# A second buffer for raw weight rows, and a residual requested later, in a two-layer MLP

## The chip, the cores and the metric

The kernel runs on 1 core of one Trainium2 chip. The metric is the device time of one execution in microseconds; the median of several runs is compared.

## The reference

The program is one post-norm layer of an encoder on x (1024 tokens x 1024, float32): layer norm, an input projection, two groups of heads (a gated DeltaNet in both directions, and 2-D neighbourhood attention), an output projection, a residual with layer norm, and a squared-ReLU MLP with the same kind of residual. The change lies in the MLP, where D_FF = 4096 and alpha = 2^(1/4):

```python
mix = jnp.einsum('bte,ed->btd', jnp.concatenate([o_gdn, o_na], axis=-1), w_out[l])
x = layer_norm(DEEPNORM_ALPHA * x + mix, ln1_g[l], ln1_b[l])
ff = jnp.square(jax.nn.relu(jnp.einsum('btd,df->btf', x, w1[l]) + b1[l]))
ff = jnp.einsum('btf,fd->btd', ff, w2[l]) + b2[l]
x = layer_norm(DEEPNORM_ALPHA * x + ff, ln2_g[l], ln2_b[l])
```

## The kernel before, in words

Every product is made of three matmuls on float32r operands, each value split into a high part (an ACT copy) and the remainder (a VectorE subtraction, `sub_split`, line 71). Both layers of the MLP are written as seven products of half-size blocks in place of eight (a Strassen scheme), so sums and differences of blocks of the weights and of the activations are operands too.

First layer, `up_pair(g)` for g = 0 to 15 (line 1044): each g takes 256 columns of w1. `w1_raw` (line 887) requests 1 MB of raw w1 rows into a `q8` buffer (two of them), two groups ahead in the program. `w_steps` (line 895) makes four sums s1 to s4 in tiles of the tag `tt` (line 870) and seven split operands in tiles of the tag `y` (line 882, eight of them). The products are p6, p7, p5, p2, p4, p3; the one in `p3` (`psF`) reuses a PSUM bank which line 1101 (`join7`, tile `u`) has to read first. The activated blocks and their four sums are written to DRAM (`h_d`, lines 1042 and 1142). Ahead of the loop, six early pieces of w1 (`w1q`, lines 958 to 961) are loaded into `tt` tiles as well.

Within the same loop the sums of w2 that the second layer needs are made, half a group at a time: `w2_load` (line 1023) requests two pieces of 256 KB into the tile `r` (named w2r), of which there is one; `w2_sums` (line 1030) makes four sums on VectorE in the tile `t` (w2s), of which there is one too, and writes them to DRAM (`t_d`, line 1036, requested by ACT).

Second layer: seven products i, each in four groups, n = 4i + gr. `down_ops(n)` (line 1153) requests 1 MB of activations and 1 MB of weights (line 1163) into a `q8` pair where n is a multiple of 3, else into one of two `big` buffers, and splits them on ACT (line 1166) and VectorE into `x` tiles (five). The `big` buffers hold operands of the first layer until its last group's p4 and p3. `down_mm` (line 1262) makes 12 matmuls of 128 x 512 for each of four row blocks, 48 in a group. `take` (line 1238) adds the results of a product into the tiles `yr`. `down_ops` stands two groups ahead of its matmuls in the loop; groups 0 and 1 are requested within the last `up_pair` (`first_ops`).

The residual: after the first layer norm x goes to DRAM (`y_d`, line 941). Lines 1183 to 1194, which stand in the program between the two layers, request five vectors broadcast to all partitions (ln1's g and b, b2, ln2's g and b) in a pool that takes the place of the first layer's work tiles, and the eight tiles of `y_d` into `yr` (tag `y`, the buffers of the first layer's split weights); VectorE then makes alpha * (g y + b) + b2 of them.

What sets the order: all these loads are issued by SP, in order, on one queue; stores of h_d and t_d by ACT on its own. The order of each engine's instructions is not that of the program text. The kernel is built with `tile.TileContext(nc, schedule_with_timeline_sim=True)` (line 1378): a planner takes, for each engine, whichever instruction its own timing says is ready (operands there, a buffer free), earlier program lines first. On the chip the order is then fixed, and each engine waits at whatever is not ready. Paced matmuls and a few `issue_after` blocks add edges by hand, none of them at the lines of this change.

Of the kernel before, what the change touches and what calls it, by code (L numbers as in the profile page):

```python
# [7 lines left out]
F32 = mybir.dt.float32  # L8
F32R = mybir.dt.float32r
AF = mybir.ActivationFunctionType  # L10
ALU = mybir.AluOpType
# [4 lines left out]
P = 128  # L16
T = 1024
DM = 1024
NK = DM // P
NT = T // P  # L20
DFF = 4096
NF = DFF // P
ALPHA = 2.0 ** 0.25
# [13 lines left out]
def tile_trunk(ctx: ExitStack, tc: tile.TileContext, A: dict, out: bass.AP):  # L37
    nc = tc.nc
    V, S, G, TE, D = nc.vector, nc.scalar, nc.gpsimd, nc.tensor, nc.sync
# [3 lines left out]
    def open_pool(name, **kw):  # L43
        opened.append(tc.alloc_tile_pool(name=name, bufs=1, **({} if kw.get("space") == DRAM else {"reuse_waits": "tile"}), **kw))
        return opened[-1]
# [24 lines left out]
    def sub_split(eng, lo, full, hi):  # L70
        return eng.tensor_tensor(lo, full, f32(hi), ALU.subtract)  # L71
# [473 lines left out]
    for i in range(8):  # L545
        for d in range(2):
            n = i if d == 0 else 7 - i
            on = oaccs[n // 4][:, n % 4]
            ld = []
            for nm, src in (("vt", vt_d), ("kT", kT_d), ("qk", qk_d[d]), ("qT", qT_d), ("kt", kt_d)):  # L550
                t = p2.tile([P, 4, P], F32, tag="l" + nm, name="l" + nm, bufs=2)
# [129 lines left out]
    yp = open_pool("yacc")  # L681
# [107 lines left out]
    def raw8():  # L789
        return op.tile([P, 2, DM], F32, tag="q8", name="wraw", bufs=2)  # L790
# [32 lines left out]
    for p in range(4):  # L823
# [11 lines left out]
        for u in units[p]:  # L835
            if u == 8:
                r = [raw8() for i in range(2)]
                wo1 = load_wo(1, [r[k // 2][:, k % 2] for k in range(4)])
            t = u % 8
# [16 lines left out]
    y_d = dr.tile([NT, P, DM], F32, name="y_d")  # L856

    xp = open_pool("xops")
    wk = open_pool("work")
# [7 lines left out]
        X[nm] = bigp.tile([P, 2, 4, 512], F32R, tag="big", name="x" + nm, bufs=2)  # L867

    def tmp(name):
        return wk.tile([P, 512], F32, tag="tt", name=name, bufs=6)  # L870

    def hold8(name):
        return wk.tile([P, 512], F32, tag="f0", name=name, bufs=8)
# [21 lines left out]
    def w_steps(raw, w):  # L895

        q11, q12, q21, q22 = (w_quad(raw, a, k) for a in range(2) for k in range(2))
        s1, s2, s3, s4 = (tmp(f"ws{i}").rearrange("p (k c) -> p k c", k=4) for i in range(4))

        def put(nm, src):  # L900
            if nm not in w:
                w[nm] = w_split(src)

        V.tensor_tensor(s1, q21, q22, ALU.add)
        put("11", q11)
        yield
        V.tensor_tensor(s2, s1, q11, ALU.subtract)
        put("S2", s2)
        yield
        V.tensor_tensor(s3, q11, q21, ALU.subtract)  # L910
        put("S3", s3)
        yield
        put("S1", s1)
        yield
        put("12", q12)
        yield
        put("22", q22)
        yield
        V.tensor_tensor(s4, q12, s2, ALU.subtract)
        put("S4", s4)  # L920
        yield
# [36 lines left out]
    for g in range(1, NE):  # L958
        for k in range(2):
            rawq[g, k] = tmp("w1q").rearrange("p (k c) -> p k c", k=4)  # L960
            D.dma_start(rawq[g, k], A["w1"][k * 512:k * 512 + 512, 2 * g * P:(2 * g + 1) * P].rearrange("(kt p) c -> p kt c", p=P))
    for hf in range(2):
        for q in range(4):
            t = hf * 4 + q
# [52 lines left out]
    w2p = open_pool("w2p")  # L1017
# [3 lines left out]
    raws1[1] = w1_raw(1)  # L1021

    def w2_load(g, hc):
        r = w2p.tile([P, 2, 2, 256], F32, tag="r", name="w2r", bufs=1)
        for k in range(2):
            D.dma_start(r[:, k], A["w2"][(2 * g + k) * P:(2 * g + k + 1) * P, :]
                        .rearrange("p (j c) -> p j c", j=2)[:, :, hc * 256:hc * 256 + 256])
        return r
# [15 lines left out]
    def up_pair(g, mid=None):  # L1044
# [11 lines left out]
        else:  # L1056
# [3 lines left out]
            S.activation(u2, pa, AF.Copy)  # L1060
        step()
        r = w2_load(g - 1, 0) if g else None
        u3 = utile("u3")
        h11, h21, h22, h12 = (hold8(x) for x in ("h11", "h21", "h22", "h12"))
# [50 lines left out]
        if g == 0:  # L1115
            pe, pf = p5(), p3()
            pc = p7()
            p6()
            join7(pc)
            join5(pe)  # L1120
            p4()
            p2()
            join3(pf)
        else:
            p6()
            join7(p7())
            join5(p5())
            w2_sums(g - 1, 0, r)
            r = w2_load(g - 1, 1)
            if mid is not None:  # L1130
                mid()
            p2()
            p4()
            w2_sums(g - 1, 1, r)
            join3(p3())
# [17 lines left out]
    def down_ops(n):  # L1153
        i, gr = divmod(n, NQ)
        sl = slice(gr * 4, gr * 4 + 4)
        if n % 3 == 0:
            raws = [raw8().rearrange("p a (k c) -> p (a k) c", c=512) for j in range(2)]
        else:
            r = bigp.tile([P, 2, 4, 512], F32, tag="big", name="d2r", bufs=2)
            raws = [r[:, j] for j in range(2)]  # L1160
        res = []
        for src, raw in zip(order[i], raws):
            D.dma_start(raw, src[:, sl])
            t = xp.tile([P, 2, 4, 512], F32R, tag="x", name="d2", bufs=5)
            for k in (slice(0, 2), slice(2, 4)):
                S.activation(t[:, 0, k], raw[:, k], AF.Copy)  # L1166
                sub_split(V, t[:, 1, k], raw[:, k], t[:, 0, k])
            res.append(t)
        ops2[n] = res
# [7 lines left out]
    for hc in range(2):  # L1177
        w2_sums(NG - 1, hc, w2_load(NG - 1, hc))
# [2 lines left out]

    fp = open_pool("fin")
    gB, bB, g2B, b2L, b2B = (fp.tile([P, DM], F32, name=x) for x in ("gB", "bB", "g2B", "b2L", "b2B"))
    for t_, nm in ((gB, "ln1_g"), (bB, "ln1_b"), (b2B, "b2"), (g2B, "ln2_g"), (b2L, "ln2_b")):
        D.dma_start(t_, A[nm].to_broadcast([P, DM]))
    V.tensor_scalar(gB, gB, ALPHA, None, ALU.mult)
    V.scalar_tensor_tensor(bB, bB, ALPHA, b2B, ALU.mult, ALU.add)
    yr = []
    for t in range(NT):
        y = yp.tile([P, DM], F32, tag="y", name="yr", bufs=8)  # L1190
        D.dma_start(y, y_d[t])
        V.tensor_tensor(y, y, gB, ALU.mult)
        V.tensor_tensor(y, y, bB, ALU.add)
        yr.append(y)
    us = [fp.tile([P, 512], F32, name=f"us{q}") for q in range(4)]
    sts = {}

# [40 lines left out]
    def take(i, q, ps):  # L1238
        y0, y1, u = yr[q], yr[4 + q], us[q]
        if i == 0:  # L1240
            S.activation(u, ps, AF.Copy)
            add(y0[:, lo_], y0[:, lo_], ps)
        elif i == 1:
            add(u, u, ps)
            add(y0[:, hi_], y0[:, hi_], u)
        elif i == 2:
            add(u, u, ps)
            add(y1[:, lo_], y1[:, lo_], u)
        elif i == 3:
            add(y0[:, hi_], y0[:, hi_], ps)  # L1250
            add(u, u, ps)
            add(y1[:, hi_], y1[:, hi_], u)
            stats(4 + q, 512, 512)
        elif i == 4:
            add(y1[:, lo_], y1[:, lo_], ps)
            stats(4 + q, 0, 512)
            finish(4 + q, 0)
        elif i == 5:
            add(y0[:, lo_], y0[:, lo_], ps)
            stats(q, 0, 512)  # L1260

    def down_mm(ps, n, q, c, start, stop):
        h, w = ops2[n]
        qs_ = slice(q * P, (q + 1) * P)
        for k in range(4):
            TE.matmul(ps, h[:, 0, k, qs_], w[:, 0, k, c], start=(start and k == 0), stop=False)  # L1266
            TE.matmul(ps, h[:, 0, k, qs_], w[:, 1, k, c], start=False, stop=False)  # L1267
            TE.matmul(ps, h[:, 1, k, qs_], w[:, 0, k, c], start=False, stop=(stop and k == 3))  # L1268

    cuts = {q: ((0, 512),) for q in range(4)}  # L1270
    for i in range(7):
        if i == 6:
            cuts[3] = ((0, 256), (256, 256))
        tags = "st" if i % 2 == 0 else "op"
        ps = {}
        for q in range(4):
            for k, (c0, cn) in enumerate(cuts[q]):
                ps[q, c0] = psC.tile([P, cn], F32, tag="o" if k else tags[q // 2], name="psdn", bufs=2)
        for gr in range(NQ):
            n = i * NQ + gr  # L1280
            if n + 2 < 7 * NQ:
                down_ops(n + 2)
            if i == 6 and gr >= NQ - 2:
                continue
            for q in range(4):
                for c0, cn in cuts[q]:
                    down_mm(ps[q, c0], n, q, slice(c0, c0 + cn), gr == 0, gr == NQ - 1)
            if gr == NQ - 1:
                for q in range(4):
                    take(i, q, ps[q, 0])  # L1290
# [91 lines left out]
```

## Time and profile before

| what | us |
|---|---|
| median of 3 runs | 1384.3 |
| the three runs | 1372.8, 1384.89, 1384.3 |
| the profiled execution, its own time | 1387.8 |
| its span, first to last instruction | 1385.8 |
| PE (matmuls) busy | 1293.7 (93%) |
| DVE (VectorE) busy | 947.9 (68%) |
| ACT (ScalarE) busy | 634.3 (46%) |
| mean DMA rate over the span | 194 GB/s |

PE busy means that matmuls are in flight, and their ends are modelled. Times in the rows are microseconds from the start of the span unless they say ns. In a timeline the columns are start, duration, engine, line, operation, tile written <- tiles read, count (xN: N merged instructions), and in brackets the idle time ahead of it and what ended it. PEclk is TensorE's granted clock as a share of full speed. Arrows in tables of waits read "who <- whom it waited for: total us, times, longest". SP's and ACT's queue entries (SPq, ACTq) are the issuing of DMAs, not the transfers.

### The profile page before, as it was taken

How to read it: one execution, taken by the hardware profiler on the slowest of the kernel's cores; microseconds unless marked ns; L12 is line 12 of the kernel's file. 1: busy time of each engine (PE TensorE's matmuls, PEld its weight loads, DVE VectorE, ACT ScalarE, POOL GpSimd, SP SyncE). 2: the span in 40 equal slices, each digit the busy share in tenths (PEclk: the TensorE clock that was granted, in tenths of full speed). 3: DMA queues.
4: the chain of work that ended last, by engine and by line, in shares of the span. 5: the costliest groups of instructions: out<-in, count | busy, mean ns of one | idle time of the engine just before them, and what ended most of it. 6: DMA issues, size and time to landing. Idle time of an engine off the chain costs nothing. (4 is left out here: it accounts for less than half of the span.)

```text
span 1385.8 us, 20027 instructions
## 1 busy us (share of the span) xinstructions
PE 1293.7 (93%) x7318; PEld 1072.5 (77%) x7318; DVE 947.9 (68%) x1707; ACT 634.3 (46%) x1224; POOL 187.8 (14%) x208
## 2 busy tenths in 40 slices
PE   5999999999999977699998899999998999999996
PEld 4688888888888866688875687777786788888885
DVE  6755797942348645757699886777875686565855
ACT  5457666434333145346366454444444433333531
POOL 3000001011113237513130000000000000000403
PEclk9999999999999999899999899999999899999998
DMA  6134548466877599565154677677779957555721
GB/s 193 51 99 126 145 122 182 124 147 202 234 224 222 135 277 329 150 173 147 45 179 134 213 257 250 208 248 259 238 267 354 396 197 246 182 182 193 257 96 61
DMA packets 242690, 268.32 MB, mean 194 GB/s; under 512 B 38928, under 2 KB 171920, under 8 KB 242592
## 3 DMA queue, kind: packets, MB, share of 16 engines
q1 hardware_dynamic: 208416, 216.70, 51.8%
q10 hardware_dynamic: 34176, 50.34, 10.4%
q8 instruction: 58, 0.95, 0.3%
q14 instruction: 40, 0.33, 0.1%
HBM read 181.99 MB, written 85.00 MB: 193 GB/s over the span
## 5 line engine op out<-in xcount | busy, mean ns | idle before, releaser
L1266 PE MATMUL psdn<-d,d 128*128 128x512 f32 (+1 forms) x464 | 175.3, 386 | 6.9 <-ACT d L1166 6.9
L1267 PE MATMUL psdn<-d,d 128*128 128x512 f32 (+1 forms) x464 | 177.9, 384 | 0.1
L1268 PE MATMUL psdn<-d,d 128*128 128x512 f32 (+1 forms) x464 | 177.6, 383 | 0.0
L71 DVE TENSOR_TENSOR d<-d2r,d 128x1024 fp32r<-128x1024 f32 x72 | 85.6, 1239 | 63.4 <-ACT d L1166 63.4
L1166 ACT ACTIVATE d<-d2r 128x1024 fp32r<-128x1024 f32 x72 | 71.3, 1048 | 109.5 <-PE psdn L1268 91.1
L1266 PEld LDWEIGHTS psdn<-d,d 128*128 128x128 f32 x464 | 88.0, 190 | 24.7 <-ACT d L1166 7.8
L1267 PEld LDWEIGHTS psdn<-d,d 128*128 128x128 f32 x464 | 87.8, 189 | 17.7 <-DVE d L71 0.6
L1268 PEld LDWEIGHTS psdn<-d,d 128*128 128x128 f32 x464 | 87.8, 189 | 17.2
L93 POOL TENSOR_TENSOR lrs<-lrs,mhalf 128x1 f32<-128x1 f32 x8 | 6.4, 806 | 615.5 <-DVE lrs L1208 615.5
L120 PE MATMUL psj<-xlo,whi 128*128 128x512 f32 x192 | 77.4, 403 | 1.9 <-DVE xlo L71 1.9
L119 PE MATMUL psj<-xhi,whi 128*128 128x512 f32 x192 | 77.0, 402 | 0.7 <-DVE xhi L170 0.7
L121 PE MATMUL psj<-xhi,wlo 128*128 128x512 f32 x192 | 76.5, 398 | 0.0
L71 DVE TENSOR_TENSOR d<-wraw,d 128x1024 fp32r<-128x1024 f32 x40 | 47.9, 1236 | 30.1 <-ACT d L1166 30.1
L1039 ACT ACTIVATE h<-h,b1T 128x512 f32<-128x512 f32 x48 | 34.7, 722 | 73.9 <-DVE h L1105 37.6
L71 DVE TENSOR_TENSOR wlo<-wraw,whi 128x1024 fp32r<-128x1024 f32 x28 | 34.3, 1223 | 47.9 <-ACT whi L110 43.3
L883 ACT ACTIVATE w1t<-ws 128x512 fp32r<-128x512 f32 x64 | 39.9, 626 | 57.9 <-DVE hs L1137 17.0
L1166 ACT ACTIVATE d<-wraw 128x1024 fp32r<-128x1024 f32 x40 | 40.0, 1049 | 55.1 <-PE psdn L1268 44.9
L240 DVE SCALAR_TENSOR_TENSOR cy<-hraw,convw,cy 128x1024 f32<-128x1024 f32 x48 | 61.2, 1281 | 5.6 <-ACT cy L238 4.5
L754 PEld LDWEIGHTS po<-vt,et 128*128 128x128 f32 x384 | 51.3, 194 | 7.9 <-ACT et L752 3.7
L743 ACT ACTIVATE ex<-sn,nm 128x384 f32<-128x384 f32 x64 | 39.0, 610 | 36.0 <-DVE nm L739 20.5
L754 PE MATMUL po<-vt,et 128*128 128x64 f32 x384 | 50.7, 271 | 4.4 <-ACT et L752 2.9
L802 PE MATMUL psop<-wo,oh 128*128 128x512 f32 x128 | 52.9, 416 | 1.6 <-ACT wo L785 1.3
(340 smaller groups left out, 3488.8 us busy)
## 6 DMA issues: line engine op xcount, KB each, us to landing
wraw<-in_w_dram SPq DMA_DIRECT2D x21, 1024.0 KB, 7.3
d2r<-h_d SPq DMA_DIRECT2D x18, 1024.0 KB, 5.5
w2r<-in_w_dram SPq DMA_DIRECT2D x64, 256.0 KB, 4.8
t_d<-w2s ACTq DMA_DIRECT2D x32, 512.0 KB, 4.8
h_d<-hs ACTq DMA_DIRECT2D x64, 256.0 KB, 2.1
wraw<-in_w_in_dram SPq DMA_DIRECT2D x28, 512.0 KB, 4.5
h_d<-h ACTq DMA_DIRECT2D x48, 256.0 KB, 5.3
d2r<-t_d SPq DMA_DIRECT2D x11, 1024.0 KB, 9.3
```

The source lines that it names most:

```text
L71: return eng.tensor_tensor(lo, full, f32(hi), ALU.subtract)
L119: pace(TE.matmul(ps, hi[:, kt], xhi[:, kt, sl], start=(kt == 0), stop=False))
L120: pace(TE.matmul(ps, hi[:, kt], xlo[:, kt, sl], start=False, stop=False))
L121: pace(TE.matmul(ps, lo[:, kt], xhi[:, kt, sl], start=False, stop=(kt == NK - 1)))
L240: V.scalar_tensor_tensor(y, raw[:, i:i + T], convw[:, ci, i:i + 1], y, ALU.mult, ALU.add)
L754: mm = TE.matmul(po[:, j], et[:, c], vts[j][:, t + c, e * 64:e * 64 + 64], start=(c == 0), stop=(c == 2))
L802: pace(TE.matmul(ps, oh[:, k], hi[k][:, c], start=(k == 0), stop=False))
L883: S.activation(t[:, 0], src, AF.Copy)
L1166: S.activation(t[:, 0, k], raw[:, k], AF.Copy)
L1266: TE.matmul(ps, h[:, 0, k, qs_], w[:, 0, k, c], start=(start and k == 0), stop=False)
L1267: TE.matmul(ps, h[:, 0, k, qs_], w[:, 1, k, c], start=False, stop=False)
L1268: TE.matmul(ps, h[:, 1, k, qs_], w[:, 0, k, c], start=False, stop=(stop and k == 3))
```

## The change

The tile of raw w2 rows gets a second buffer (4 KB per partition); to make room the tag `tt` goes from six tiles to four (2 KB each). The residual's eight loads, the three vectors that they are combined with and the arithmetic move into a function, called in the second layer's loop at n == 1, after `down_ops(3)`; ln2's two vectors are requested at n == 8. The tiles `yr` are still allocated where they were.

```diff
     def tmp(name):
-        return wk.tile([P, 512], F32, tag="tt", name=name, bufs=6)
+        return wk.tile([P, 512], F32, tag="tt", name=name, bufs=4)
...
     def w2_load(g, hc):
-        r = w2p.tile([P, 2, 2, 256], F32, tag="r", name="w2r", bufs=1)
+        r = w2p.tile([P, 2, 2, 256], F32, tag="r", name="w2r", bufs=2)
...
     gB, bB, g2B, b2L, b2B = (fp.tile([P, DM], F32, name=x) for x in ("gB", "bB", "g2B", "b2L", "b2B"))
-    for t_, nm in ((gB, "ln1_g"), (bB, "ln1_b"), (b2B, "b2"), (g2B, "ln2_g"), (b2L, "ln2_b")):
-        D.dma_start(t_, A[nm].to_broadcast([P, DM]))
-    V.tensor_scalar(gB, gB, ALPHA, None, ALU.mult)
-    V.scalar_tensor_tensor(bB, bB, ALPHA, b2B, ALU.mult, ALU.add)
-    yr = []
-    for t in range(NT):
-        y = yp.tile([P, DM], F32, tag="y", name="yr", bufs=8)
-        D.dma_start(y, y_d[t])
-        V.tensor_tensor(y, y, gB, ALU.mult)
-        V.tensor_tensor(y, y, bB, ALU.add)
-        yr.append(y)
+    yr = [yp.tile([P, DM], F32, tag="y", name="yr", bufs=8) for t in range(NT)]
+
+    def residual():
+        for t_, nm in ((gB, "ln1_g"), (bB, "ln1_b"), (b2B, "b2")):
+            D.dma_start(t_, A[nm].to_broadcast([P, DM]))
+        V.tensor_scalar(gB, gB, ALPHA, None, ALU.mult)
+        V.scalar_tensor_tensor(bB, bB, ALPHA, b2B, ALU.mult, ALU.add)
+        for t, y in enumerate(yr):
+            D.dma_start(y, y_d[t])
+            V.tensor_tensor(y, y, gB, ALU.mult)
+            V.tensor_tensor(y, y, bB, ALU.add)
+
...
             if n + 2 < 7 * NQ:
                 down_ops(n + 2)
+            if n == 1:
+                residual()
+            if n == 8:
+                for t_, nm in ((g2B, "ln2_g"), (b2L, "ln2_b")):
+                    D.dma_start(t_, A[nm].to_broadcast([P, DM]))
```

## Rows read from the trace of the kernel before

**Rows 1.** Busy time by stretch: PE, PEld, DVE, ACT, POOL, then PEclk, DMA, GB/s.
```profile
740.00:760.00 20.00, 13.81 (x53) 9.11 (x51) 20.00 (x37) 11.64 (x21) 0.00 (x0) 0.94 0.39 113
...
1160.00:1200.00 40.00, 40.00 (x179) 33.11 (x178) 21.35 (x23) 13.02 (x14) 0.00 (x0) 1.00 0.60 208
```

**Rows 2.** What PE waited for, 725 to 1140 us.
```profile
PE psF L925 <- DVE u L1101: 9.0, 9, 2.1
PE psdn L1266 <- ACT d L1166: 6.7, 1, 6.7
```

**Rows 3.** PE's timeline where the second layer's second group begins.
```profile
1068.84 0.39 PE L1268 MATMUL psdn<-d,d 128*128 128x512 f32 x1
1075.89 2.07 PE L1266 MATMUL psdn<-d,d 128*128 128x512 f32 x4 [6.67 <-ACT d L1166]
...
1081.18 0.63 PE L1266 MATMUL psdn<-d,d 128*128 128x512 f32 x1
1081.61 0.53 PE L1267 MATMUL psdn<-d,d 128*128 128x512 f32 x1
```

**Rows 4.** Busy time in one stretch of 4 us there, columns as in rows 1.
```profile
1076.00:1080.00 4.00, 4.00 (x10) 3.13 (x11) 2.38 (x3) 1.11 (x2) 0.00 (x0) 0.50 1.05 406
```

**Rows 5.** SP's timeline of DMA requests between the layers.
```profile
1043.02 9.51 SPq L1191 DMA_DIRECT2D yr<-y_d  x5
1056.46 1.21 SPq L1026 DMA_DIRECT2D w2r<-in_w_dram  x2
1057.76 0.94 SPq L1191 DMA_DIRECT2D yr<-y_d  x1
1058.83 0.42 SPq L1163 DMA_DIRECT2D d2r<-h_d  x1
1059.29 0.98 SPq L1163 DMA_DIRECT2D d2r<-in_w_dram  x1
1061.29 1.52 SPq L1191 DMA_DIRECT2D yr<-y_d  x2
...
1087.80 0.93 SPq L1185 DMA_DIRECT2D gB<-in_ln_g_dram  x1
```

**Rows 6.** ACT's timeline, the splits of groups n = 1 and 2.
```profile
1072.65 1.06 ACT L1166 ACTIVATE d<-d2r 128x1024 fp32r<-128x1024 f32 x1 [5.57 <-DMA d2r<-in_w_dram]
...
1083.35 2.01 ACT L1166 ACTIVATE d<-d2r 128x1024 fp32r<-128x1024 f32 x2 [1.67 <-DMA d2r<-in_w_dram]
```

**Rows 7.** DMA issues by line: count, KB each, median us to landing.
```profile
w2r<-in_w_dram SPq DMA_DIRECT2D x64, 256.0 KB, 4.8
t_d<-w2s ACTq DMA_DIRECT2D x32, 512.0 KB, 4.8
...
yr<-y_d SPq DMA_DIRECT2D x8, 512.0 KB, 7.2
```

**Rows 8.** Instructions by tile, first and last start: w2r's requests; psE's matmuls.
```profile
L1026 SPq DMA_DIRECT2D w2r<-in_w_dram x64: 539/608/1742, 712.6 to 1057.1; - x64
...
L925 PE MATMUL psE<-xT,w1t x64: 387/389/403, 742.0 to 1047.7; 128*128 128x512 f32 x64
```

**Rows 9.** VectorE's timeline: the residual's arithmetic, and its first reader.
```profile
1113.93 9.17 DVE L1192 TENSOR_TENSOR yr<-yr,gB 128x1024 f32<-128x1024 f32 x8
...
1141.17 2.48 DVE L1236 TENSOR_TENSOR yr<-yr,psdn 128x512 f32<-128x512 f32 x4
```

**Rows 10.** What VectorE waited for, 765 to 1060 us.
```profile
DVE ws L904 <- DMA wraw<-in_w_dram: 29.9, 12, 5.1
DVE w2s L1032 <- DMA w2r<-in_w_dram: 17.2, 13, 2.7
...
DVE w2s L1032 <- DMA t_d<-w2s: 5.7, 2, 3.5
```

**Rows 11.** The early pieces of w1: their ACT splits, and landing after request.
```profile
L883 ACT ACTIVATE w1t<-w1q x6: 615/632/637, 715.0 to 733.2; 128x512 fp32r<-128x512 f32 x6
...
DMA to landing us min/median/max: 3.1/4.3/5.1
```

## The prediction

> **What bounds the kernel now.** I read the busy time by stretch first, then TensorE's waits, then the timelines of PE, SP and ACT where the largest wait stands, then VectorE's waits. In the second layer PE has no gap to close from 1160 to 1360 us, five stretches of 40 us of which one stands in the rows: busy 40.00 of 40, 179 matmuls, one every 0.2235 us [rows 1]. Nothing in the diff takes a matmul away, so a gain can come only from where PE is idle. Between 725 and 1140 us the diff's lines reach two such idle times [rows 2]: 6.7 us in one piece in front of the second layer's second group (groups are counted n = 0, 1, 2, ... as in `down_ops`), and 9.0 us in nine pieces in front of the first layer's seventh product, `psF`, which waits for VectorE's `u` (line 1101). The stretch from 740 is a third: DVE is busy 20.00 of 20 us there, PE 13.81 [rows 1].
>
> The one piece: the last matmul of n = 0 starts at 1068.84, the next at 1075.89, 6.67 us idle, and then matmuls come every 0.43 us up to the one at 1081.61 [rows 3]; the granted clock is 0.50 in 1076 to 1080 [rows 4], the lower of the two levels (1.2 of 2.4 GHz), after PE had stood still. That is some 14 matmuls at 0.43 - 0.22 = 0.21 us extra, 2.9 us. The whole event is worth 6.7 + 2.9 = 9.5 us. Its cause stands on ACT: the first split of n = 1 starts at 1072.65, after 5.57 us of waiting for the DMA of its weights [rows 6]; they were requested at 1059.29 [rows 5]. In those 13.4 us the DMA engines are full (share 1.05, 406 GB/s [rows 4]), so it is bytes, not latency: 13.4 x 0.406 = 5.4 MB went by, 2.1 MB of them this pair. Ahead of and beside it stand the eight residual requests of 1043.02 to 1062.8 [rows 5], 512 KB each [rows 7]: 4.2 MB, 10.3 us of a full DMA.
>
> **The change part by part.**
>
> *Residual later.* If all eight requests really go behind the loads of n = 3, n = 1 lands up to 10.3 us earlier; 6.67 are needed. What is late next is n = 2: its weights land at 1083.35 [rows 6] and PE follows a landing by 1075.89 - 1072.65 = 3.2 us, so 1086.6, while n = 1, if on time, ends at 1069.2 + 48 x 0.2235 = 1079.9. It too needs 6.7 us, and has the same 10.3. So the full 9.5 us would go. But the order on a queue is not the program's: line 1378 has a planner order each engine's instructions by when its own timing says that they are ready. The w2 rows' first request is at 712.6, though the first product of the first layer's main loop that precedes it in the program (`psE`) runs at 742.0 [rows 8]; so a request is pulled forward, there by 30 us, past work that stands before it. A residual request needs only a free `y` buffer, and those come free with the last group of the first layer whatever stands at n == 1. The like holds for ln2's two vectors, moved to n == 8. I therefore take it as likelier that most of the eight still go out around 1043 to 1062.
>
> What then still moves is SP: before, the w2r request of 1056.46 had to wait for the one buffer, and n = 1's pair stood behind it and behind a sixth residual request (1057.76) until 1058.83 [rows 5]. With two buffers that w2r request is out before the residual, and the pair can follow the fifth residual request, which ends at 1043.02 + 9.51 = 1052.5, as soon as its buffer is free; one to three residual pieces (0.5 to 1.6 MB, 1.3 to 3.9 us) fall behind it. One w2r piece and one t_d piece, 1.05 MB or 2.6 us, leave the crowded stretch, since the chain of w2 sums runs a step further ahead. Sum 3.9 to 6.5 us of the 6.67 needed; I take 5, which leaves 1.7 at n = 1. At n = 2 only the 2.6 us count (the residual is still ahead of it), against 6.7 - 1.7 = 5.0: 2.4 left, and I put 1 us for the clock. So 9.5 - 5.1 = 4.4 us gained. Ends: 9.5 gained, 0 gained.
>
> The Trainium skill, "DMA: Bandwidth & Descriptors", section "Rules for kernel authors", speaks against a later request: issue a DMA early, compute, wait late. The trace shows what the early request buys: the residual is asked for from 1043.02 and first read by VectorE at 1113.93 [rows 5, 9], so some 40 us of earliness are unused; by that rule the move would cost, by the rows it costs nothing until the landing passes 1113.9.
>
> *Residual's arithmetic.* The same instructions on DVE (two on the vectors, eight products that take 9.17 us from 1113.93, eight additions of the same size), before the first eviction that needs them at 1141.17 [rows 9]: 18.3 of 27.2 us. They stay beside PE's work: 0. If they move to where operands are scarce they can hold back the splits; end: one more event like that of 1069, +9.5.
>
> *Two w2r buffers.* VectorE, in order, waits 17.2 us in 13 places for w2r, in the same queue as `u`, and 29.9 us in 12 places for w1's raw rows; for t_d, whose tile still has one buffer, 5.7 us [rows 10]. The load and the store of one half start together when its sums are done, and both have a median landing of 4.8 us [rows 7]. So the removed wait has a successor: the next sums now wait for the `w2s` tile instead. Where load and store land nearly together, only a part of the 17.2 goes; I take half, 8 to 9 us of DVE time. What PE gets of it is bounded by the nine waits, 9.0 us; the w1 waits remain and are the larger part of the cause. 17.2 / (17.2 + 29.9) of 9.0 is 3.3; I take 3. Ends: 0 and 9.0. On the losing side, if stores land later than today's loads, +5.7, today's whole wait for t_d once more.
>
> *Four `tt` tiles for six.* In the main loop a group takes four of them in turn and each is done with before its successor is written: 0. At the start, six early pieces of w1 share them (split from 715.0 to 733.2, 4.3 us from request to landing [rows 11]); with four, the last two must be requested after the first splits, about 719, and land 4.3 us later, some 10 us ahead of their own split. Cover: DVE is the bound here. It also keeps the planner from running the next group's sums ahead of the operands PE waits for from 740 on [rows 1]. Ends: +4.3 (that landing, uncovered) and -5; I take 0.
>
> **Sum** for the profiled execution (1387.8 us; span 1385.8 and 2.0 around it): -4.4 - 3 + 0 = -7.4, so 1380.4. The median of the runs shown is 3.5 us below that execution; against it 1384.3 - 7.4 = 1377.
>
> **The rivals.**
> A. The residual really goes behind the operands of n = 1 to 3: -9.5 - 3 = -12.5, 1372. For it: the program's place. Against it: the pulling forward in [rows 8].
> B. Both idle times go, psF's too: -9.5 - 9.0 = -18.5, 1366. For it: both have one cause, a DMA late for an in-order engine. Against it: the w1 waits, which the diff leaves.
> C. Nothing: DMA is full from before n = 1 to after n = 2 in any order, and t_d's wait replaces w2r's: 1384.
> D. Slower. The residual lands in the middle of the second layer: its 4.2 MB with three vectors of 0.5 MB (requested from 1087.80 [rows 5] before) form one block of 5.8 MB, 14 us at 0.406, in front of a pair of n = 3 to 6. A group lasts 10.7 us, so a pair that is requested less than about 14 + 3 + 5 (its own 2.1 MB) = 22 us ahead, two groups, stalls PE; from that point on it costs what the stall at 1069 costs, 9.5, and DVE held by the residual's first product waiting for its vector adds as much again at worst. With the old stall gone and 3 gained elsewhere: +9.5 + 9.5 - 9.5 - 3 = +6.5, 1391; with the old stall kept, 1397 to 1400.
>
> The Trainium skill, same page, section "Specifications", gives about 358 GB/s of HBM per core. The row shows 406 [rows 4]; at 358 the block of D would be an estimated 16 us and D likelier. The measurement decides.
>
> **How the numbers follow.** Forecast 0.38 (own range 1373 to 1381), A 0.22, B 0.12, C 0.10, D 0.18. The range goes 2 us past B, for the clock after psF's nine stops, which B does not price, and leaves out the worse half of D: 1364 to 1392. About 1%, 13.8 us, is what a measurement can tell here (the runs shown differ by 12). Faster by more: nearly all of B, a third of A, a little of the forecast, 0.23; slower by more: half of D, 0.10; else 0.67.
>
> **What would show it.** Right: SP's timeline has w2r requests ahead of all yr, n = 1's pair before 1057; the idle time before `psdn` near 1069 is under 4 us in all with the granted clock back at 1.00 sooner; DVE's wait for w2r is below 4 us and that for t_d above 5.7. A is shown by yr requests after those of n = 3. Wrong: the 6.7 us stall unchanged, psF's 9.0 us unchanged or larger, or a new idle time of PE after 1090, where it now has none.

## The result, and the profile after

After: 1361.92 us, the median of 16 runs (1357.11 to 1374.19); before 1382.26 (1372.8 to 1388.24, 16 runs). The ratio is 0.987, 95% interval [0.9845, 0.9894]: 18 us faster, 1.3%. Forecast were 1377 us and, as likeliest, a change within 1%. The median lies 2 us under the range; the ratio, put on the 1384.3 us of the forecast, gives 1366 (1363 to 1370), its lower end.

The profiled execution took 1361.37 us (span 1359.3), 26.4 less than that of before. Not all of that is the change. The row of attention's scores (the second `pss` product, with its first and last start) in before, after, and a second profile of the changed kernel:

```profile
L736 PE MATMUL pss<-kl,qs x64: 338/341/522, 492.7 to 671.3; 128*128 128x384 f32 x64
```
```profile
L736 PE MATMUL pss<-kl,qs x64: 337/341/525, 493.2 to 659.4; 128*128 128x384 f32 x64
```
```profile
L736 PE MATMUL pss<-kl,qs x64: 337/341/525, 493.6 to 670.9; 128*128 128x384 f32 x64
```

Up to there the instructions of before and after stand in the same order on every engine, and still the same program ends this part at 659.4 or at 670.9. So kernels are compared below by the stretch from the last `pss` to the end of the span: 714.5 us before (1385.8 - 671.3), 699.9 and 699.6 in the two profiles of after. That is 14.6 us for the diff to explain. Two profiles of one kernel, the two-buffer one below, differ in this stretch by 3.7 us, so parts of that size are not told apart.

What PE waited for in after, 690 to 1120 us (us in total, times, longest):

```profile
...
PE psdn L1268 <- DVE d L71: 3.6, 1, 3.6
PE psdn L1267 <- ACT d L1166: 2.7, 2, 1.4
...
PE psF L925 <- DVE u L1101: 0.5, 1, 0.5
```

What VectorE waited for there:

```profile
DVE w2s L1032 <- DMA t_d<-w2s: 28.7, 14, 7.3
...
DVE ws L904 <- DMA wraw<-in_w_dram: 3.1, 3, 2.4
DVE w2s L1032 <- DMA w2r<-in_w_dram: 0.5, 1, 0.5
```

Against [rows 2, 10]: `psF`'s nine stops are one of 0.5. The wait for w2r has become one for t_d, as forecast. The wait for w1's raw rows, 29.9 us, which the forecast left standing, is 3.1. At the boundary of the layers the stop has moved more than shrunk. After's timeline of SP there:

```profile
1016.10 14.23 SPq L1192 DMA_DIRECT2D yr<-y_d  x6
1030.42 0.52 SPq L1163 DMA_DIRECT2D d2r<-h_d  x1
1037.16 0.38 SPq L1163 DMA_DIRECT2D d2r<-in_w_dram  x1
```

Its timelines of VectorE, ACT and PE, one line of each:

```profile
1027.75 0.42 DVE L1032 TENSOR_TENSOR w2s<-w2r 128x256 f32<-128x256 f32 x1 [7.27 <-DMA t_d<-w2s]
```
```profile
1029.84 1.06 ACT L1166 ACTIVATE d<-wraw 128x1024 fp32r<-128x1024 f32 x1 [7.71 <-DVE w2s L1034]
```
```profile
1035.04 0.80 PE L1268 MATMUL psdn<-d,d 128*128 128x512 f32 x1 [3.60 <-DVE d L71]
```

Its busy time in the stretch of that stop, columns as in [rows 1]:

```profile
1030.00:1040.00 10.00, 4.94 (x11) 3.28 (x12) 8.60 (x12) 4.19 (x6) 0.00 (x0) 0.66 1.01 350
```

Six of the eight residual requests still go out ahead of n = 1's pair, at 1016.10 (before: six too, five from 1043.02 and one at 1057.76 [rows 5]). Beside them a store of w2's sums is slow, VectorE stands 7.27 us for it, ACT's next split of n = 0 behind VectorE, and PE behind that: n = 0 is late now, not n = 1. From 340 to 460 us behind the last `pss`, PE's idle time and the clock's shortfall (60 us times what the granted clock lacks) come to 7.9 + 5.4 us before and 6.9 + 3.6 after. So the boundary gave 2.9 of the 14.6 us in this pair of profiles, the first layer most of the rest: from 71 to 290 us behind that mark idle time went from 18.4 to 10.8 and the clock from 0.96 to 0.97. Before, above, and after, below:

```profile
742.30:961.30 219.00, 200.57 (x841) 159.31 (x840) 175.84 (x321) 102.09 (x175) 0.00 (x0) 0.96 0.70 228
```
```profile
730.40:949.40 219.00, 208.21 (x885) 167.80 (x884) 186.93 (x344) 108.56 (x183) 0.00 (x0) 0.97 0.75 249
```

### The profile page after: what moved, and what is told of

Same layout as the page of the kernel before. It is cut to its first block, busy times and chain, and to the rows that moved or that the text cites. A ratio compares the mean times of both kernels' runs of the same rounds, so it can differ in the third digit from the quotient of the medians.

```text
span 1359.3 us, 20056 instructions
## 1 busy us (share of the span) xinstructions
PE 1293.3 (95%) x7318; PEld 1074.7 (79%) x7318; DVE 937.8 (69%) x1707; ACT 636.0 (47%) x1224; POOL 188.4 (14%) x208
## 5 line engine op out<-in xcount | busy, mean ns | idle before, releaser
L1269 PEld LDWEIGHTS psdn<-d,d 128*128 128x128 f32 x464 | 87.4, 188 | 16.8
```

## The experiments

Ratios are to before, run on the same chip. The waits are those of 690 to 1120 us; "last sum" is the last start of line 1032 less the first start of `psdn`. Its first product runs while the first layer still ends, so a plus means that w2's sums run on into the second layer.

| kernel | ratio | stretch us | psF stops | VectorE for w1 rows / w2r / t_d | last sum |
|---|---|---|---|---|---|
| before | 1 | 714.5 | 9.0 | 29.9 / 22.0 / 7.0 | +7.6 |
| after | 0.987 | 699.9 | 0.5 | 3.1 / 0.5 / 28.7 | -3.2 |
| after, the second profile | 0.9868 | 699.6 | 0.5 | 4.5 / under 1 / 25.3 | -3.2 |
| two w2r, four tt | 0.9898 | 697.5 | 0 | 3.1 / 3.5 / 17.9 | -8.5 |
| the same again | 0.9887 | 701.2 | 0.5 | 2.0 / 4.2 / 22.1 | -3.2 |
| residual moved alone | 0.9995 | 713.4 | 7.3 | 26.4 / 24.3 / 7.2 | +7.8 |
| four tt alone | 0.9925 | 700.4 | 4.0 | 2.1 / 34.1 / 5.6 | -17.7 |
| before, s1 held | 1.0027 | 712.6 | 8.5 | under 1 / 38.4 / 14.9 | +7.5 |
| before, s1 and s4 held | 0.9917 | 703.7 | 3.8 | under 1 / 39.0 / 8.4 | -36.7 |
| before, s4 held | 0.9873 | 694.8 | 0 | under 1 / 23.9 / 8.4 | -3.8 |
| after, w2s doubled, not w2r | 1.0118 | 733.1 | 24.1 | 4.0 / 77.1 / under 1 | -6.4 |
| after, residual held | 0.9911 | 704.4 | 1.0 | 3.6 / 1.8 / 24.9 | -6.5 |
| both of these | 1.0173 | 742.1 | 25.5 | 3.9 / 78.4 / under 1 | -7.0 |
| after, residual spread | 0.9855 | 695.2 | 0.9 | 3.9 / 5.2 / 16.8 | -7.2 |

**The buffer edits without the residual.**

```diff
-        return wk.tile([P, 512], F32, tag="tt", name=name, bufs=6)
+        return wk.tile([P, 512], F32, tag="tt", name=name, bufs=4)
...
-        r = w2p.tile([P, 2, 2, 256], F32, tag="r", name="w2r", bufs=1)
+        r = w2p.tile([P, 2, 2, 256], F32, tag="r", name="w2r", bufs=2)
```

> Before, with the second buffer for w2r and four tt tiles; the residual keeps its old place. Times are ratios to before, beside the stretch from the start of the last pss to the end of the span (before 714.8 us, after 700.2). Theory 1, the buffer is what paid, by an order of work in the first layer in which VectorE no longer waits for w1's raw rows: psF's 9.0 us of stops fall below 2, VectorE's wait for w1's raw rows from 29.9 to about 3, the stretch is 704 to 706, the ratio 0.990 to 0.993. Theory 2, the moved residual paid: psF's stops stay at 9, the ratio is 0.998 to 1.002. Theory 3, the profiled pair differs mostly by how the attention part happened to run: the ratio is over 0.995 whatever the waits show.

0.9898 [0.9829, 0.9966], and once more beside after on one chip:

> The kernel with the two buffer edits alone (two w2r, four tt, the residual in its old place) once more, since it had four executions: against after on the same chip it shows what the moved residual is worth. If nothing: within 0.003 of after, 0.985 to 0.990. By the profiled pair (697.5 against 699.9 us from the last pss) after is slower by 0.002.

> The changed kernel itself, on the same chip as the two others. 0.985 to 0.990 as before; its attention part, whose instructions are in the same order as in before, shows by how much one profile differs from another: the last pss starts at 659 to 672 us.

0.9887 [0.9837, 0.9936], after 0.9868 [0.9808, 0.9929]; stretches 701.2 and 699.6. By the first pair of profiles after was the slower of the two, by the second the faster. The two buffer edits are worth what the whole change is worth, within what these runs tell apart.

**The residual's move alone.**

```diff
-    for t in range(NT):
-        y = yp.tile([P, DM], F32, tag="y", name="yr", bufs=8)
-        D.dma_start(y, y_d[t])
...
+            if n == 1:
+                residual()
```

> Before, with the residual written at n == 1 and ln2's vectors at n == 8; one w2r buffer, six tt tiles. Theory 1: psF's stops stay at about 9 us, only the boundary of the layers changes; the residual requests still go out ahead of n = 2's pair, the stop ahead of n = 1 is 3 to 7 us, the ratio 0.996 to 1.001. Theory 2, the moved residual paid: the stop ahead of n = 1 shrinks to under 2 us and the ratio is 0.987 to 0.992.

0.9995 [0.9955, 1.0034]. Its waits of PE:

```profile
PE psF L925 <- DVE u L1101: 7.3, 9, 2.1
PE psdn L1267 <- ACT d L1166: 6.9, 1, 6.9
```

Its timeline of SP:

```profile
1041.03 10.10 SPq L1192 DMA_DIRECT2D yr<-y_d  x5
1054.26 1.22 SPq L1026 DMA_DIRECT2D w2r<-in_w_dram  x2
1055.57 1.02 SPq L1192 DMA_DIRECT2D yr<-y_d  x1
1056.71 0.42 SPq L1163 DMA_DIRECT2D d2r<-h_d  x1
```

The requests stand on SP as they did in [rows 5], and the 6.9 us stop is the old one. The text of the program moved, the queue did not, and the edit is worth nothing.

**Four tt tiles alone** (the first of the two lines above).

> Before, with four tt tiles for six and nothing else. Theory 1: no change, ratio 0.997 to 1.003, psF's stops at 7 to 11 us. Theory 4, the four tiles paid, because they bind the planner's order of VectorE's sums so that s1 of the next group no longer stands ahead of the hs sums: psF's stops below 2 us, the wait for w1's raw rows near 3, ratio 0.990 to 0.994.

0.9925 [0.9889, 0.9961], stretch 700.4: the edit that the forecast put at 0 brings 14.1 of the 14.6 us of the profiled stretch. Theory 1 falls. Half of `psF`'s stops are left, and the wait for w1's rows is 2.1 us although nothing was done to w1's buffers.

**Which order pays?** Tiles five and six let VectorE's sums of w1's rows start earlier. Three kernels leave all buffers as before and only hold such a sum back.

```diff
-        V.tensor_tensor(s1, q21, q22, ALU.add)
+        with tc.issue_after(lasths[-1].ins) if lasths else nullcontext():
+            V.tensor_tensor(s1, q21, q22, ALU.add)
```

> Before, with one edge added: the first sum of a group's w1 rows (s1, line 904) is issued behind the last hidden-layer sum (s4) written before it. Buffers and residual as before. If psF's nine stops come from s1 waiting for w1's raw rows in front of work that is ready: they fall below 3 us, VectorE's wait at s1 from 29.9 to under 10, the ratio is 0.990 to 0.996 though w2r has one buffer and VectorE still waits some 17 us for it. If the wait for w2r is what stops psF: stops of 6 us and more remain and the ratio is 0.998 or above; the fixed order may also cost where s1 had been early, over 1.002.

1.0027 [0.9989, 1.0066]. The wait for w1's rows is gone, and nothing is gained: VectorE stands for w2r and t_d instead (38.4 and 14.9 us), and `psF` stops for 8.5. The explanation from which this test came, s1 standing in front of the hs sums, falls.

```diff
+        with tc.issue_after(lastj3[-1].ins) if lastj3 else nullcontext():
+            V.tensor_tensor(s4, q12, s2, ALU.subtract)
```

Both edges together:

> Before, with two edges and nothing else: s1 of the next group's w1 rows is issued behind the last hs sum written before it, and s4 (line 919) behind the add that evicts psF (line 1111). Buffers as before: six tt, one w2r; the residual in its old place. That is about the order in which VectorE takes these sums in the kernel with four tt tiles. Theory 4a, four tiles pay because they change this order: psF's stops fall below 5 us, the wait for w1's raw rows below 10, the stretch from the last pss to the end is 699 to 706 us (before 714.5, four tiles 700.4), the ratio 0.989 to 0.995. Rival, the order of these two sums is not it (s1 alone moved nothing, 1.0027): stops of 7 us and more, stretch 711 to 716, ratio 0.998 to 1.004.

0.9917 [0.9879, 0.9955], stretch 703.7: an order alone gives what four tiles give.

The edge on s4 alone:

> Before, with the one edge on s4 (line 919 behind the add that evicts psF) and none on s1, which then stands between s4 and the hs sums, so ahead of them, as in before. The two edges together gave 0.9917 and a stretch of 703.7 us, s1's alone 1.0027 and 712.6. If s4's place is what pays (it keeps the w2 sums, behind which it had been pulled, from falling a half group later each time): the last w2 sum starts before 1030 us, before the second layer's first matmul, the stretch is 700 to 706, the ratio 0.988 to 0.995. If both sums must leave their places: VectorE still waits over 15 us for w1's raw rows at s1, the stretch is 709 to 715, the ratio over 0.997.

0.9873 [0.9811, 0.9935], stretch 694.8, better than the 700 to 706 expected: the whole gain of the change from one edge, with one w2r, six tt and the residual in its old place. The planner orders everything behind an edge anew, so more moves than s4 alone. What the edge does to the wait for w1's rows stands in SP's and VectorE's timelines. Before, first SP's request for a group's raw rows, then the s1 that reads them:

```profile
878.16 0.37 SPq L889 DMA_DIRECT2D wraw<-in_w_dram  x1
```
```profile
886.86 0.69 DVE L904 TENSOR_TENSOR ws<-wraw 128x512 f32<-128x512 f32 x1 [5.12 <-DMA wraw<-in_w_dram]
```

With s4 held, the request of 870.38 is read by the s1 of 891.24; s4, the last reader of the buffer, ends just ahead of the next request:

```profile
870.38 0.37 SPq L889 DMA_DIRECT2D wraw<-in_w_dram  x1
...
891.39 0.37 SPq L889 DMA_DIRECT2D wraw<-in_w_dram  x1
```
```profile
890.63 0.69 DVE L920 TENSOR_TENSOR ws<-wraw,ws 128x512 f32<-128x512 f32 x1
891.24 0.68 DVE L904 TENSOR_TENSOR ws<-wraw 128x512 f32<-128x512 f32 x1
```

8.7 us from request to first read before, 20.9 here, 13.0 in after (877.58 to 890.57). The order of VectorE's instructions in the built programs, with the buffers' numbers (`wraw_8779` takes the place of `wraw_8429`), says why (shortened, with a note behind each; the number in front is its place). Before, above, and s4 held, below:

```
1007 L919 ws3_8624<-wraw_8429      s4
1019 L904 ws0_8796<-wraw_8604      s1 of the next rows
1037 L71  w1t_8718<-wraw_8429      split
1041 L71  w1t_8738<-wraw_8429      split, last reader
1047 L904 ws0_8971<-wraw_8779      6 places later

1032 L71  w1t_8718<-wraw_8429      split
1037 L71  w1t_8738<-wraw_8429      split
1040 L920 ws3_8624<-wraw_8429      s4, last reader
1041 L904 ws0_8796<-wraw_8604      s1 of the next rows
1071 L904 ws0_8971<-wraw_8779      31 places later
```

Before, the sums of the next rows had begun while these rows still waited for their splits. Both raw buffers were taken nearly all the time, and this load was asked for six instructions ahead of its use. In order, a buffer is free a whole group (some 30 instructions) ahead. With four tt tiles the sums can't run so far ahead; in after the same two instructions stand at 1041 and 1057. That four tiles gain through this order is read from the programs; no run gave four tiles the old order.

An earlier load is not by itself what pays. With s1 alone held the rows are asked for earlier still: over the last 14 groups the median from request to first read is 28.8 us there, 18.6 with s4 held, 10.3 in after and 7.8 before. The first layer, from 71 to 290 us behind the last `pss`, with s1 alone held (above) and s4 alone held (below), columns as before:

```profile
729.40:948.40 219.00, 204.13 (x862) 162.01 (x861) 177.30 (x324) 103.45 (x178) 0.00 (x0) 0.98 0.72 233
```
```profile
744.30:963.30 219.00, 212.10 (x905) 170.66 (x904) 189.44 (x350) 113.15 (x190) 0.00 (x0) 0.98 0.77 253
```

VectorE is busy 177.30 us in the one, hardly more than the 175.84 before, and 189.44 in the other. What goes with the gain is the sum of VectorE's three waits in the table: 58.9 us before, 57.9 and 53.3 in the two kernels that gained nothing, 24.5 to 47.4 in those that gained, 81.1 and 82.3 in the two that lost. (With two w2r tiles another 7 to 11 us ahead of w2's sums have no releaser in the profile; counted in, the sums of those kernels stay below 42.) In these kernels an order paid where VectorE stood less in all, for whichever load. This compares profiles; it was not varied by itself.

The second effect is in the table's last column. Where VectorE stands less in all, w2's sums keep up: before they ran 7.6 us into the second layer, in every kernel that gained they end before it (in the two with w2s doubled too, which lost in the first layer). With s1 alone held they don't (+7.5), and that kernel gained nothing. That the sums must end before the boundary was not varied by itself.

**The second buffer to w2s instead, and the residual held.**

```diff
-        r = w2p.tile([P, 2, 2, 256], F32, tag="r", name="w2r", bufs=2)
+        r = w2p.tile([P, 2, 2, 256], F32, tag="r", name="w2r", bufs=1)
...
-        t = w2p.tile([P, 4, 256], F32, tag="t", name="w2s", bufs=1)
+        t = w2p.tile([P, 4, 256], F32, tag="t", name="w2s", bufs=2)
```

> After, with the second buffer given to w2s, the tile of the finished sums, and one left to w2r, the raw rows. VectorE's wait for t_d (28.7 us after) falls below 3 and that for w2r rises from 0.5 to 25 to 40 us. If the two buffers do the same work from two sides, the ratio is 0.985 to 0.991 and psF's stops stay below 3 us. If the raw rows' buffer is the better one, because a request that waits for its buffer holds up SP's queue, it is 0.990 to 0.994 with stops of 3 to 5 us, as with four tt tiles alone.

1.0118 [1.0072, 1.0165]: slower than before, and outside both expectations. Against four tt tiles alone (0.9925), from which it differs by the second w2s and the moved residual, it is 1.9% slower. Its waits of PE, then of VectorE:

```profile
PE psF L925 <- DVE u L1101: 24.1, 11, 4.2
```
```profile
DVE w2s L1032 <- DMA w2r<-in_w_dram: 76.0, 27, 6.1
```

VectorE stands for w2r in 27 of 32 places. One of them: the rows are requested at 875.26, and VectorE stands for them from 877.03 to 881.52. Again a spare tile (w2s here) lets a sum be put where its operand has hardly been asked for; that it is the same cause as with tt is argued from the pattern, no edge was tried here.

```diff
+            with tc.issue_after(dload[7].ins):
+                D.dma_start(y, y_d[t])
```

> After, with the eight residual requests held on SP behind the requests of n = 3's weights, so that they are late in fact and not only in the program. If the residual's bytes are what still holds the second layer's first groups: PE's idle time ahead of psdn falls from 6.3 us (3.6 and 2.7) to under 2, the stretch from the last pss to the end from 699.9 to 693 to 697, the ratio to before is 0.982 to 0.985. Rival, other bytes or the w2 sums hold these groups: 4 us and more stay, ratio 0.986 to 0.990. Third, the residual's 4.2 MB stall a later group instead: a new stop of PE of 3 us or more behind n = 3, ratio over 0.990.

0.9911 [0.9877, 0.9945], 0.004 above after, which the intervals don't separate; the stretch is 4.5 us longer. The old stops are gone (0.4 and 1.0 us left) and a greater one has come, at n = 2. VectorE's last hs sum, then ACT's timeline, PE's, and the busy time there:

```profile
1054.86 0.68 DVE L1140 TENSOR_TENSOR hs<-h,hs 128x512 f32<-128x512 f32 x1
```
```profile
1065.00 7.87 ACTq L1142 DMA_DIRECT2D h_d<-hs  x4
1072.91 3.90 ACT L1167 ACTIVATE d<-d2r 128x1024 fp32r<-128x1024 f32 x4 [21.07 <-DMA h_d<-hs]
```
```profile
1075.92 2.07 PE L1269 MATMUL psdn<-d,d 128*128 128x512 f32 x4 [10.38 <-ACT d L1167]
```
```profile
1060.00:1070.00 10.00, 5.54 (x25) 4.25 (x23) 0.00 (x0) 0.00 (x0) 0.00 (x0) 0.97 1.04 404
1070.00:1080.00 10.00, 4.08 (x10) 3.18 (x11) 6.00 (x6) 7.08 (x8) 0.00 (x0) 0.51 1.04 406
```

The hs sums were ready at 1055.5, but ACT got rid of their four stores only from 1065.00 to 1072.87, and the splits of n = 2 stand behind the stores on ACT. The wait list of each store names, beside VectorE, one of eight DMA semaphores that all requests of SP and ACT share; seven residual requests had gone out since 1052.86. The trace's semaphore events say which transfer each store waited for: they were released at 1064.92, 1066.20, 1067.48 and 1072.47, by the landing of n = 2's own weights (requested at 1052.30) and then of three residual requests (1052.86, 1055.80, 1058.18). None of the four stores needs these data; each signals its own landing on the semaphore that it waited for.

Before had the same at its old stop. ACT stood at a store of finished data,

```profile
1072.28 0.33 ACTq L1142 DMA_DIRECT2D h_d<-hs  x1
```

released at 1072.21 by the landing of n = 1's weights. The split behind it, at 1072.65 [rows 6], reads the activations, which had landed at 1069.15; the first split of the weights starts only at 1074.78, 2.6 us after they landed.

> The two edits together: the second buffer for w2s, and the residual's requests held behind n = 3's. If both causes are separate the ratio is the product of the two steps against after, so within 0.003 of (held run's ratio) x (w2s run's ratio) / 0.987. If the request for w2r that waits for its one buffer stands on SP ahead of n = 1's pair again, the stop ahead of n = 1 is back at 4 us or more and the ratio is over 0.988.

1.0173 [1.0121, 1.0224]; the product would be 1.016, so the runs fit two separate effects; the stop is at n = 2 (10.9 us), not at n = 1.

**The residual spread.**

```diff
+        for y, src in [(yr[t], y_d[t]) for t in (2 * m, 2 * m + 1)]:
+            with tc.issue_after(dload[9 + 2 * m].ins):
+                D.dma_start(y, src)
...
+            if 2 <= n <= 5:
+                residual(n - 2)
```

> After, with the residual's requests spread: two behind the weights of each of n = 4, 5, 6 and 7, the vectors behind n = 4's, ln2's two behind n = 10's. If requests that go out within some 10 us share the DMA engines whatever their order on the queue (the held run's pair of 1051.65 landed 20 us later, with seven residual requests behind it), then neither the store of w2's sums nor a pair is slowed any more: PE's idle time ahead of psdn at n = 1 to 3 is under 2.5 us in all (after 6.3, held 10.8), the stretch from the last pss to the end is 691 to 695 us (after 699.9), the ratio 0.979 to 0.984. Rival, the products of the residual come too late for the first eviction or the splits behind them: a stop of 3 us or more at the end of n = 3, ratio over 0.986.

0.9855 [0.9807, 0.9904], after on the same chip 0.9868: the times don't tell them apart. The expected 0.979 to 0.984 did not come. The expectation also misread the held run: there no pair of d2r took over 12.7 us to land, it was ACT that stood. In the profile the stretch is 695.2 against 699.6 and 699.9, and t_d's stores between 1005 and 1035 us land sooner (after, where the landing of one of three is known, then the spread residual):

```profile
DMA to landing us min/median/max: 10.7/10.7/10.7
```
```profile
DMA to landing us min/median/max: 3.4/4.1/6.2
```

That the residual ahead of the boundary costs some 4 us is therefore not shown: two profiles of one kernel differ by 3.7.

## Why the forecast came out as it did

- **What bounds the kernel:** right. Most of what was gained came from PE's idle time, and the clock beside it, in the places named; from 1120 to 1160 us after is busy 40.00 of 40, as in [rows 1].
- **Four tt tiles, taken as 0:** the step that failed. "In the main loop a group takes four of them in turn and each is done with before its successor is written" is true of the tiles, and beside the point: tiles five and six were what let the sums run ahead. The prediction did see that four tiles keep the planner from running the next group's sums ahead, but only for the stretch from 740 us on, with 5 us as its end, and took 0. Alone, the edit measured 0.9925, some 10 us (5 to 15): the order changes in every group of the first layer.
- **"The w1 waits remain", "which the diff leaves":** wrong for the same reason. 29.9 us went to 3.1. On this sentence the w2r term was set at a third of 9.0 us and rival B got 0.12. B's condition (psF's stops go) came true, and its price, 1366, is what the ratio gives; but the edge on s4 brings it with one w2r buffer, so not through the cause that B named. That the range held the ratio is luck: its lower end stands there for B's price, while the forecast itself was 1377 and its likeliest case a change within 1%.
- **Two w2r buffers, -3:** not resolved. With four tt tiles the second buffer takes `psF`'s last stops (4.0 to 0 and 0.5 us); the stretch moves by 1 us (700.4 to a mean of 699.4) and the ratio by 0.003 to 0.004, within the intervals. With six tt it wasn't tried: the two don't fit in memory together. That t_d's wait takes its place was right (7.0 to 28.7 us).
- **Boundary, -4.4:** the profile shows -2.9, but the two profiles of the two-buffer kernel lose 6.7 and 11.5 us there, so a term of this size is not told from 0. That the residual would still be pulled ahead was right (1016.10, six requests), and its move alone measured nothing (0.9995). The earlier w2r requests (last one at 1010.7, before at 1057.1 [rows 8]; behind the last `pss`, 351.3 and 385.8 us) come from the sums that keep up; four tiles alone already take the loss there from 13.3 to 6.3 us (4.5 idle, 1.8 clock). The old stop was also not all bytes: by the store at 1072.28, shown with the held run, an estimated 2.6 of its 6.67 us were ACT's order. And the 13.4 us ahead of that landing moved 362 GB/s, 4.8 MB; the 406 of [rows 4] belong to the 4 us that follow it.
- **Rival A:** its premise was made true by force. The ratio to before, 0.9911, is its price of 1372, but by luck: its boundary term of -9.5 came out as a loss of 3.9 us more than before (17.2 against 13.3), and what it gained came from the first layer. It counted the bytes ahead of a pair and left out the requests themselves, which hold back other requests, ACT's stores among them. The rule quoted there (issue early, wait late, in the Trainium skill's "DMA: Bandwidth & Descriptors", "Rules for kernel authors") is not decided by this kernel: requested late in one block the residual measured 0.9911, spread over four groups 0.9855, early 0.987, and the intervals overlap.
- **Rival D:** a stop of about its size came in the held kernel (10.4 us, priced at 9.5), but at n = 2 and through ACT's stores, not through a late pair of n = 3 to 6; in the change itself nothing of it came.
- **What would show it:** the w2r requests ahead of all yr, the pair before 1057 and the two waits of VectorE came as written. The idle time before `psdn`, to be under 4 us in all, was 6.3.

## What to carry to other kernels

A tile's buffer count is also a leash on the order: where a scheduler fills in-order engines, one buffer more can let work run ahead that keeps another buffer taken, and taking two away was worth 0.75% here (given to the wrong tile, one more cost 2%). So price a change in a buffer count by asking who reads each operand last, how far ahead of its use its load can then be requested, and whether the in-order engine behind the stops then stands less in all or only for another load. And read the queue, not the program: a request that is moved in the text and not held by an edge may go out when it did before.

## What the runs showed that was not expected

- The same instructions in the same order ended attention's part at 659.4 or 670.9 us in different profiles: PE's wait there for VectorE's `nm` was 9.9 us in one and 19.9 in the other. One profiled pair may differ by 12 us for that alone, and the 16 runs of before and of after spread by 15 and 17.
- A DMA request can hold the engine that issues it: ACT stood for 21.07 us around four stores of finished data while the DMA engines moved 404 to 406 GB/s. It stood for the landing of four other transfers, three of them of the residual, which had the stores' semaphores.
